# Gate and up of 17 of 22 feed-forward blocks in seven half-size products; the inner rows in four parts

## The chip, the cores and the metric

The kernel runs on one core of one Trainium2 chip. The metric is the device time of one launch in microseconds. A core has five engines that run side by side and meet through semaphores: TensorE (PE, matrix products; the loading of its weights is shown apart as PEld), VectorE (DVE), ScalarE (ACT), GpSimd (POOL) and SyncE (SP), which here issues nearly all transfers. Each takes its instructions in program order. TensorE writes its products into PSUM; Vector and Scalar read them there.

## The reference, cut to what matters

A decoder trunk of two layers, one with a convolution and one with attention, is run for 512 new prompt tokens and 8 x 8 sample tokens, 576 columns in all. Each layer ends in a gated feed-forward part, which is all that the change touches:

```python
def swiglu(x, g, w_gate_up, w_down):
    gu = rms_norm(x, g) @ w_gate_up
    return (jax.nn.silu(gu[..., :D_FF]) * gu[..., D_FF:]) @ w_down
```

The model width is 1024 (8 k-tiles of 128) and D_FF is 2816, 22 blocks of 128 inner rows. All data is float32. The prompt and the sample tokens go through the same weights.

## The kernel before, in words

Activations lie transposed: features on the 128 partitions, the N = 576 tokens in the free dimension, taken in two halves of HN = 288. TensorE multiplies in a faster reduced format, so each factor is split into a high part and the rest (`split`, L270: ScalarE copies x into hi, Vector subtracts to get lo), and each k-tile of a product is three matmuls, hi x hi, hi x lo, lo x hi (`mm3`, L227 to L230).

Weights come as a stream in the order of use (`specs`, L104). `w_load` (L110) starts a transfer into one of two raw buffers. `w_split` (L130) takes the oldest raw block and queues its splitting into whi and wlo, two buffers of each; `w_work` (L157) issues queued pieces to ScalarE (L140) and Vector (L141). `w_next` (L161) hands out the oldest split block, starts a load, puts out up to two background cache copies of 1 MB on SP (`bg_copy`, L180, on average 1.5 a call) and splits the next block. The order of the work on each engine is the order in which the program writes it: the kernel asks for a manual schedule and no planner moves anything.

`ffn` (L772) runs once per layer. In each of two halves, eleven blocks are multiplied: a gate product and an up product (`proj`, L274) of 8 k-tiles x 2 token halves x 3 matmuls = 48 matmuls each. The input uh/ul is x times its norm weight; the factor by token, `rs`, is known only after the first block, so every block's result is multiplied by it as it leaves PSUM:

```python
nc.vector.tensor_mul(halves(t), pg, halves(rs))      # L795
nc.scalar.activation(s, t, AF.Silu)                  # L797
nc.vector.tensor_mul(halves(t2), pu, halves(rs))     # L799
nc.vector.tensor_mul(t2, t2, s)                      # L800
split(hh[:, f], hl[:, f], t2)                        # hi on ScalarE, lo on Vector
```

Then the half's eight down products (11 k-tiles, 66 matmuls each) are added into the residual xT (L810). In the last half `after` prepares the next stage column tile by column tile: `x_fill` in layer 0, the transposed output `y_rows` in layer 1. PSUM is used as four tiles of two banks.

Of the kernel before, what the change touches and what calls it, by code (L numbers as in the profile page):

```python
# [34 lines left out]
KT = 8  # L35
# [4 lines left out]
N = S + NS  # L40
# [4 lines left out]
GH = 3072  # L45
DFF = 2816
FT = DFF // 128
TAPS = 31
EPS = 1e-6
SC = HD ** -0.5  # L50
# [40 lines left out]
def trunk(ctx: ExitStack, tc: tile.TileContext, I, O, dbg=None):  # L91
# [12 lines left out]
    def spec(ap, shape, scale=None):  # L104
        specs.append((ap, shape, scale))

    wstate = {"raw": [], "ready": [], "n": 0, "rate": 1.5, "lo": nc.vector, "cut": 4}
    BUFR, BUFH = 2, 2

    def w_load():  # L110
        if not specs:
            return
        ap, shape, scale = specs.pop(0)
        raw = wpool.tile([128, WSLOT], F32, tag="wraw", name="wraw", bufs=BUFR)
        n = int(np.prod(shape))
        v = raw[:, :n]
        if len(shape) == 2:
            v = v.rearrange("p (a b) -> p a b", a=shape[0])
        else:
            v = v.rearrange("p (a b c) -> p a b c", a=shape[0], b=shape[1])  # L120
        if len(shape) == 2:
            nc.sync.dma_start(v, ap)
        else:
            for j in range(shape[1]):
                nc.sync.dma_start(v[:, :, j], ap[j])
        wstate["raw"].append((raw, n, shape, scale))

    parts = []

    def w_split(cut=None):  # L130
# [5 lines left out]
        hi = wpool.tile([128, WSLOT], F32R, tag="whi", name="whi", bufs=BUFH)  # L136
        lo = wpool.tile([128, WSLOT], F32R, tag="wlo", name="wlo", bufs=BUFH)

        def plain(c):
            nc.scalar.activation(hi[:, c], raw[:, c], AF.Copy)  # L140
            wstate["lo"].tensor_sub(lo[:, c], raw[:, c], hi[:, c].bitcast(F32))  # L141

        def scaled(k, m):
            c = slice(k * m, (k + 1) * m)
            nc.scalar.activation(hi[:, c], raw[:, c], AF.Copy, scale=scale[:, k:k + 1])
            nc.vector.scalar_tensor_tensor(lo[:, c], raw[:, c], scale[:, k:k + 1],
                                           hi[:, c].bitcast(F32), op0=ALU.mult, op1=ALU.subtract)
# [12 lines left out]

    def w_next(lazy=False):  # L161
        w_work()
        while not wstate["ready"]:
            if not wstate["raw"]:
                w_load()
            w_split()
            w_work()
        r = wstate["ready"].pop(0)
        if not lazy:
            w_load()  # L170
        bg_copy()
        w_split()
        if not lazy:
            w_work()
        return r
# [11 lines left out]
    def col_blocks(w, k0, nk, c0, nc_):  # L187
        return w[k0 * 128:(k0 + nk) * 128, c0:c0 + nc_].rearrange("(k p) n -> p k n", p=128)
# [6 lines left out]

    def ffn_specs(l):
        wg, wd = I["w_gate_up"][l], I["w_down"][l]
        for hf in range(2):
            for f in range(hf * 11, hf * 11 + 11):
                spec([col_blocks(wg, 0, KT, f * 128, 128), col_blocks(wg, 0, KT, DFF + f * 128, 128)], (KT, 2, 128))  # L200
            for m in range(KT):
                spec(col_blocks(wd, hf * 11, 11, m * 128, 128), (11, 128))

    ffn_specs(0)

# [26 lines left out]
    def halves(ap):  # L232
        return ap.rearrange("p (h n) -> p h n", h=2)
# [36 lines left out]
    def split(hi, lo, x):  # L270
        nc.scalar.activation(hi, x, AF.Copy)  # L271
        nc.vector.tensor_sub(lo, x, hi.bitcast(F32))
# [499 lines left out]
    def ffn(l, u, before_last, after, late=0):  # L772
        with ExitStack() as cx:
            big = cx.enter_context(tc.tile_pool(name=f"f_big{l}", bufs=1))
            wk = cx.enter_context(tc.tile_pool(name=f"f_wk{l}", bufs=2))
            ps = cx.enter_context(tc.tile_pool(name=f"f_ps{l}", bufs=4, space=PSUM, reuse_waits="tile"))
            rs = big.tile([128, N], F32, name="rs")
            hh = big.tile([128, 11, N], F32R, name="hh")
            hl = big.tile([128, 11, N], F32R, name="hl")
            ks = [(k, k) for k in range(KT)]  # L780
            for hf in range(2):
                for f in range(11):
                    wh, wl = w_next()
                    if hf == 0 and f == 0:

                        pg, pu = (x[:, :, :HN] for x in pair(ps, [wh[:, :, i] for i in range(2)],
                                                             [wl[:, :, i] for i in range(2)], u.uh, u.ul))
                    else:
                        pg = proj(ps, wh, wl, u.uh, u.ul, ks, lambda w, k: w[:, k, 0])
                        pu = proj(ps, wh, wl, u.uh, u.ul, ks, lambda w, k: w[:, k, 1])  # L790
                    if hf == 0 and f == 0:
                        rstd_bc(ps, wk, u.acc, rs)
                        nc.scalar.activation(u.acc[:, 0:1], u.acc[:, 0:1], AF.Silu)
                    t = wk.tile([128, N], F32, name="gt")
                    nc.vector.tensor_mul(halves(t), pg, halves(rs))  # L795
                    s = wk.tile([128, N], F32, name="sg")
                    nc.scalar.activation(s, t, AF.Silu)  # L797
                    t2 = wk.tile([128, N], F32, name="gt2")
                    nc.vector.tensor_mul(halves(t2), pu, halves(rs))  # L799
                    nc.vector.tensor_mul(t2, t2, s)  # L800
                    split(hh[:, f], hl[:, f], t2)
                if hf:
                    u.close()
                    before_last()
                for m in range(KT):
                    wh, wl = w_next()
                    pt = proj(ps, wh, wl, hh, hl, [(k, k) for k in range(11)], lambda w, k: w[:, k])
                    if hf and late and m:
                        after(ps, wk, m - 1)
                    nc.vector.tensor_add(halves(xT[:, m]), halves(xT[:, m]), pt)  # L810
                    if hf and not late:
                        after(ps, wk, m)
                if hf and late:
                    after(ps, wk, KT - 1)


# [779 lines left out]
```

## Time and profile before

| | |
|---|---|
| median of 3 runs | 2066.39 us (2065.44 to 2069.13) |
| the profiled execution: its own time | 2061.0 us |
| its span, first to last instruction | 2059.1 us |
| mean granted TensorE clock | 0.98 |
| matmuls | 17109 |
| gate and up matmuls behind each layer's first block | 4032 (3 x 1344) |
| down matmuls | 2112 (3 x 704) |

The profile's first part gives each engine's busy time, share of the span and count. A group row gives line, engine, operation, output and inputs, shape and count, then the total busy time in us and the mean of one in ns, then the idle time before it and what ended it. A timeline row begins with its start in us from the start of the span and its length in us; matmuls overlap, so their length is not their pitch. A row of stretches gives, for each engine, the busy time and the number of instructions, then the clock, the DMA share and GB/s.

### The profile page before, as it was taken

Reading aid. Unit: us, or ns where it says so; the run is one execution under the profiler, and the core shown is the slowest. Engines: PE = TensorE matmul, PEld = TensorE weight load, DVE = VectorE, ACT = ScalarE, POOL = GpSimd, SP = SyncE. Lnnn points to the kernel's source line nnn. Section 1 sums busy time; section 2 is a strip of 40 time slices with the busy share of each in tenths; the row PEclk is TensorE's granted clock in tenths of the full one; section 3 lists DMA queues with packets and bytes.
Section 4 is the critical chain, followed back from the end, with each engine's and each line's share of the span. In section 5 each row is a group of like instructions: output and inputs, shape, how many; then the busy total and the mean of one; then the engine's idle time right before and its main releaser. Section 6 shows DMA issues by size and latency. Waiting matters only on the chain.

```text
span 2059.1 us, 40751 instructions
## 1 busy us (share of the span) xinstructions
PE 1950.8 (95%) x17109; PEld 1801.3 (87%) x17109; DVE 1013.1 (49%) x1922; ACT 810.7 (39%) x1836; POOL 159.9 (8%) x292
## 2 busy tenths in 40 slices
PE   6989799999999999999999999988897999999999
PEld 6767499999999999998888888866566999999998
DVE  5776665432444486564455356325454454324432
ACT  6554633221222343444344344266564332112221
POOL 1000000000000033130122032000112000000000
PEclk9999899999999999999999999989898999999999
DMA  7430196568655856759778887699979555643222
GB/s 211 144 143 22 34 322 224 197 213 292 204 197 189 290 165 198 212 171 259 209 212 230 246 230 211 205 227 220 205 160 249 202 203 197 217 117 82 76 71 75
DMA packets 368873, 387.81 MB, mean 188 GB/s; under 512 B 17983, under 2 KB 357975, under 8 KB 367010
## 3 DMA queue, kind: packets, MB, share of 16 engines
q1 hardware_dynamic: 368130, 384.06, 62.4%
q8 instruction: 135, 2.21, 0.5%
q0 software_dynamic: 560, 1.14, 0.2%
q14 instruction: 48, 0.39, 0.1%
HBM read 348.07 MB, written 146.86 MB: 240 GB/s over the span
## 4 chain that ended last, share of the span: by engine, by line
PE 84%; DMA 6%; ACT 5%; DVE 3%; SPq 1%; issue 1%; another core or an unknown queue 0%; ACTq 0%; DVEq 0%
PE pmm L230 13%; PE pmm L229 13%; PE pmm L228 13%; PE pj L228 7%; PE pj L229 7%; PE pj L230 7%; PE pj L1191 3%; PE tp L964 3%; PE acc L558 3%; PE pmp L229 2%; PE pmp L230 2%; PE pmp L228 2%; DMA nat<-scr 2%; PE pv L1062 2%; PE tp L989 2%; DMA vv<-in_cache_kv_w_dram 1%
## 5 line engine op out<-in xcount | busy, mean ns | idle before, releaser
L230 PE MATMUL pmm<-uh,wlo 128*128 128x288 f32 x1344 | 396.2, 295 | 0.0
L228 PE MATMUL pmm<-uh,whi 128*128 128x288 f32 x1344 | 395.9, 295 | 0.0
L229 PE MATMUL pmm<-ul,whi 128*128 128x288 f32 x1344 | 395.7, 294 | 0.0
L228 PE MATMUL pj<-whi,xh 128*128 128x256 f32 x1152 | 332.0, 288 | 0.9 <-DVE xT L810 0.9
L229 PE MATMUL pj<-wlo,xh 128*128 128x256 f32 x1152 | 322.3, 280 | 0.0
L230 PE MATMUL pj<-whi,xl 128*128 128x256 f32 x1152 | 322.1, 280 | 0.0
L228 PEld LDWEIGHTS pmm<-uh,whi 128*128 128x128 f32 x1344 | 252.1, 188 | 0.1
L229 PEld LDWEIGHTS pmm<-ul,whi 128*128 128x128 f32 x1344 | 252.1, 188 | 0.1
L230 PEld LDWEIGHTS pmm<-uh,wlo 128*128 128x128 f32 x1344 | 252.1, 188 | 0.0
L228 PEld LDWEIGHTS pj<-whi,xh 128*128 128x128 f32 x1152 | 217.2, 189 | 10.3 <-issue 9.5
L140 ACT ACTIVATE whi<-wraw 128x1024 fp32r<-128x1024 f32 (+3 forms) x206 | 169.2, 872 | 123.0 <-PE pmm L229 100.6
L229 PEld LDWEIGHTS pj<-wlo,xh 128*128 128x128 f32 x1152 | 217.2, 189 | 0.0
L230 PEld LDWEIGHTS pj<-whi,xl 128*128 128x128 f32 x1152 | 216.7, 188 | 0.0
L141 DVE TENSOR_TENSOR wlo<-wraw,whi 128x1024 fp32r<-128x1024 f32 (+3 forms) x206 | 197.7, 1003 | 23.3 <-ACT whi L140 23.0
L228 PE MATMUL pmm<-hh,whi 128*128 128x288 f32 x704 | 207.6, 295 | 0.0
L230 PE MATMUL pmm<-hh,wlo 128*128 128x288 f32 x704 | 207.5, 295 | 0.0
L229 PE MATMUL pmm<-hl,whi 128*128 128x288 f32 x704 | 207.2, 294 | 0.0
L799 DVE TENSOR_TENSOR gt<-pmm,rs 128x576 f32<-128x576 f32 x42 | 31.8, 757 | 224.6 <-PE pmm L230 224.6
L271 ACT ACTIVATE hh<-gt 128x576 fp32r<-128x576 f32 x44 | 30.2, 686 | 263.3 <-DVE gt L800 263.3
L229 PEld LDWEIGHTS pmm<-hl,whi 128*128 128x128 f32 x704 | 132.1, 188 | 0.0
L228 PEld LDWEIGHTS pmm<-hh,whi 128*128 128x128 f32 x704 | 132.1, 188 | 0.0
L230 PEld LDWEIGHTS pmm<-hh,wlo 128*128 128x128 f32 x704 | 132.0, 188 | 0.0
(295 smaller groups left out, 3518.3 us busy)
## 6 DMA issues: line engine op xcount, KB each, us to landing
out_dram<-in_cache_kv_w_dram SPq DMA_DIRECT2D x64, 1016.0 KB
wraw<-in_w_gate_up_dram SPq DMA_DIRECT2D x88, 512.0 KB
out_dram<-in_cache_kv_w_dram SPq DMA_DIRECT2D x32, 1008.0 KB
wraw<-in_w_kv_dram SPq DMA_DIRECT2D x24, 1024.0 KB
wraw<-in_w_down_dram SPq DMA_DIRECT2D x32, 704.0 KB
kk<-in_cache_kv_w_dram SPq DMA_DIRECT2D x40, 512.0 KB
vv<-in_cache_kv_w_dram SPq DMA_DIRECT2D x40, 512.0 KB
scr<-r SPq DMA_DIRECT2D x36, 512.0 KB
```

The lines of the kernel that those rows point to most:

```text
L140: nc.scalar.activation(hi[:, c], raw[:, c], AF.Copy)
L141: wstate["lo"].tensor_sub(lo[:, c], raw[:, c], hi[:, c].bitcast(F32))
L228: nc.tensor.matmul(out, wh, xh, start=start, stop=False)
L229: nc.tensor.matmul(out, wh, xl, start=False, stop=False)
L230: nc.tensor.matmul(out, wl, xh, start=False, stop=stop)
L271: nc.scalar.activation(hi, x, AF.Copy)
L558: nc.tensor.matmul(acc[r][32 * (j - m):32 * (j - m) + 32], DG[c][g, j], exf[c][g, j:S + j], start=m == 0, stop=j + 4 >= TAPS)
L799: nc.vector.tensor_mul(halves(t2), pu, halves(rs))
L964: nc.tensor.transpose(pt[:, j * 128:(j + 1) * 128], Z["k", n][:, j, i * 128:(i + 1) * 128], ident)
L989: nc.tensor.matmul(pt[32 * bi:32 * bi + 32, a:a + n], q[:, x, i, b], kn[:, x, i, T * b:T * b + T] if k is None else k[:, i, bi], start=i = ...
L1062: nc.tensor.matmul(pvt[r], ph[:n, ti, r], v[:n, bi], start=ti == 0, stop=ti == 9)
L1191: nc.tensor.matmul(pt[:, :CW], xs[:, k], x[:, k], start=k == 0 and x is wh, stop=k == KT - 1 and x is wl)
```

## The change

The weight matrix of a block is seen as 2 x 2: gate and up by k-tiles 0 to 3 and 4 to 7; the input as 2 x 2: k-tiles 0 to 3 and 4 to 7 by token halves h0 and h1. The four results (gate and up, h0 and h1) are formed from seven products of half size, 12 matmuls each, in place of eight. Four sums of weight blocks and four sums of input blocks go into them. Partial results are shared by leaving them in a PSUM bank, copying the bank to SBUF with ScalarE (p1, p5, u2, u3) and adding the next product into the same bank.

The 22 blocks of a layer become quarters of 5, 6, 6 and 5, each followed by its own part of the down products, and so hh and hl hold six blocks in place of eleven. The first quarter runs as before (`plain`); beside its blocks 1 to 4 the input sums th/tl are made. The sums mix token halves, so the input has to carry `rs` beforehand: beside the first quarter's down products `rescale` rewrites uh and ul. The other 17 blocks run as `seven`. A weight block then splits into seven pieces of 512 columns, four in one pair of buffers and three (`w_tail`) in the next, so one block takes both pairs. Down weights come as nf k-tiles by 256 columns, two output tiles a load. The lo parts of hh are kept pending in `pend` and issued by `flush`.

```diff
+QUARTERS = [(0, 5), (5, 6), (11, 6), (17, 5)]
...
+    def w_tail():
+
+        if wstate["tail"] is not None:
+            w_work()
+            raw, sw, e = wstate["tail"]
+            wstate["tail"] = None
+            hi, lo = w_slot()
+            split(hi[:, :1024], lo[:, :1024], sw[:, 1024:])
+            split(hi[:, 1024:1536], lo[:, 1024:1536], raw[:, 1536:])
+            e += [hi, lo]
...
+        if scale == "seven":
+
+            r = [raw[:, i * 512:(i + 1) * 512] for i in range(4)]
+            sw = wstate["sums"]()
+            t = [sw[:, i * 512:(i + 1) * 512] for i in range(4)]
+            add, sub = nc.vector.tensor_add, nc.vector.tensor_sub
+            parts.extend([partial(add, t[0], r[2], r[3]), partial(sub, t[1], t[0], r[0]), partial(sub, t[2], r[0], r[2]),
+                          partial(sub, t[3], r[1], t[1]),
+                          partial(split, hi[:, :1024], lo[:, :1024], raw[:, :1024]),
+                          partial(split, hi[:, 1024:], lo[:, 1024:], sw[:, :1024])])
+            e = [hi, lo]
+            wstate["tail"] = (raw, sw, e)
+            wstate["ready"].append(e)
+            return
...
+    def w_take():
+
+        w_work()
+        r = wstate["ready"].pop(0)
+        w_load()
+        bg_copy()
+        return r
...
+        for f0, nf in QUARTERS:
+            for f in range(f0, f0 + nf):
+                spec([col_blocks(wg, 0, KT, f * 128, 128), col_blocks(wg, 0, KT, DFF + f * 128, 128)], (2, KT, 128),
+                     "seven" if f0 else None)
+            for m in range(0, KT, 2):
+                spec(col_blocks(wd, f0, nf, m * 128, 256), (nf, 256))
...
+            def input_sums(j):
+                za = wk.tile([128, N], F32, tag="sg", name="za")
+                zb = wk.tile([128, N], F32, tag="gt2", name="zb")
+                normed(za, j, slice(0, N))
+                normed(zb, j + 4, slice(0, N))
+                t = sums_tile()[:, :4 * HN].rearrange("p (a b) -> p a b", a=4)
+                nc.vector.tensor_sub(t[:, 0], za[:, h1], za[:, h0])
+                nc.vector.tensor_sub(t[:, 1], zb[:, h1], t[:, 0])
+                nc.vector.tensor_sub(t[:, 2], zb[:, h1], za[:, h1])
+                nc.vector.tensor_sub(t[:, 3], zb[:, h0], t[:, 1])
+                nc.scalar.activation(th[:, :, j], t, AF.Copy)
+                pend.append(lambda: nc.vector.tensor_sub(tl[:, :, j], t, th[:, :, j].bitcast(F32)))
+
+            def rescale(ks):
+
+                for k in ks:
+                    c = h0 if k < 4 else slice(0, N)
+                    z = wk.tile([128, N], F32, tag="sg", name="zs")
+                    normed(z[:, c], k, c)
+                    nc.scalar.activation(u.uh[:, k, c], z[:, c], AF.Copy)
+                    flush()
+                    pend.append(lambda k=k, c=c, z=z: nc.vector.tensor_sub(u.ul[:, k, c], z[:, c],
+                                                                           u.uh[:, k, c].bitcast(F32)))
+                flush()
...
+            def seven(i):
+
+                wxh, wxl, wyh, wyl = w_take()
...
+                direct(a, wxh, wxl, 0, 0, h0, True, False)
+                nc.scalar.activation(sn["p1"], a, AF.Copy)
+                direct(b, wxh, wxl, 1, 4, h0, True, True)
+                nc.vector.tensor_add(s[:, h0], sn["p1"], b)
+                nc.scalar.activation(s[:, h0], s[:, h0], AF.Silu)
+                summed(c, wxh, wxl, 2, 0, True, False)
+                nc.scalar.activation(sn["p5"], c, AF.Copy)
+                summed(a, wxh, wxl, 3, 1, False, False)
+                nc.scalar.activation(sn["u2"], a, AF.Copy)
+                w_split()
+                w_work(4 if wstate["tail"] is not None else 0)
+                flush()
+                w_work(1)
+                summed(a, wyh, wyl, 0, 2, False, False)
+                nc.scalar.activation(sn["u3"], a, AF.Copy)
+                nc.vector.tensor_add(t2[:, h1], sn["u3"], sn["p5"])
+                w_work()
+                direct(c, wyh, wyl, 1, 4, h1, False, True)
+                nc.vector.tensor_add(s[:, h1], sn["u2"], c)
+                nc.scalar.activation(s[:, h1], s[:, h1], AF.Silu)
+                summed(a, wyh, wyl, 2, 3, False, True)
+                nc.vector.tensor_mul(t2[:, h1], t2[:, h1], s[:, h1])
+                nc.vector.tensor_mul(t2[:, h0], s[:, h0], a)
+                w_tail()
+                nc.scalar.activation(hh[:, i], t2, AF.Copy)
+                pend.append(lambda: nc.vector.tensor_sub(hl[:, i], t2, hh[:, i].bitcast(F32)))
...
+                if last:
+                    flush()
+                    tpool.__exit__(None, None, None)
                     u.close()
                     before_last()
-                for m in range(KT):
+                for m0 in range(0, KT, 2):
                     wh, wl = w_next()
...
+                    flush()
+                    if not q:
+
+                        rescale([[0, 1], [2, 3, 4], [5, 6, 7], []][m0 // 2])
+                    for m in (m0, m0 + 1):
+                        pt = proj(ps, wh, wl, hh, hl, [(k, k) for k in range(nf)],
+                                  lambda w, k: w[:, k, 128 * (m - m0):128 * (m - m0) + 128])
...
+                        nc.vector.tensor_add(halves(xT[:, m]), halves(xT[:, m]), pt)
...
+                    w_tail()
```

`direct` multiplies the input itself and `summed` the input sums; both issue 12 matmuls, four k-tiles of three.

More of the change, by code (lines that the diff above doesn't have):

```diff
@@ L105, in spec @@
         specs.append((ap, shape, scale))
-    wstate = {"raw": [], "ready": [], "n": 0, "rate": 1.5, "lo": nc.vector, "cut": 4}
+    wstate = {"raw": [], "ready": [], "n": 0, "rate": 1.5, "lo": nc.vector, "cut": 4, "tail": None}
     BUFR, BUFH = 2, 2
@@ L123, in w_load, with w_slot @@
         else:
-            for j in range(shape[1]):
-                nc.sync.dma_start(v[:, :, j], ap[j])
+            for j, a in enumerate(ap):
+                nc.sync.dma_start(v[:, j] if shape[0] == 2 else v[:, :, j], a)
         wstate["raw"].append((raw, n, shape, scale))
     parts = []
+    def w_slot():
+        return [wpool.tile([128, WSLOT], F32R, tag=t, name=t, bufs=BUFH) for t in ("whi", "wlo")]
+    def w_tail():
[7 more added lines that the diff above has]
+            e += [hi, lo]
     def w_split(cut=None):
@@ L135, in w_split @@
         raw, n, shape, scale = wstate["raw"].pop(0)
-        hi = wpool.tile([128, WSLOT], F32R, tag="whi", name="whi", bufs=BUFH)
-        lo = wpool.tile([128, WSLOT], F32R, tag="wlo", name="wlo", bufs=BUFH)
+        hi, lo = w_slot()
+        if scale == "seven":
[11 more added lines that the diff above has]
+            return
         def plain(c):
@@ L197, in ffn_specs @@
         wg, wd = I["w_gate_up"][l], I["w_down"][l]
-        for hf in range(2):
-            for f in range(hf * 11, hf * 11 + 11):
-                spec([col_blocks(wg, 0, KT, f * 128, 128), col_blocks(wg, 0, KT, DFF + f * 128, 128)], (KT, 2, 128))
-            for m in range(KT):
-                spec(col_blocks(wd, hf * 11, 11, m * 128, 128), (11, 128))
+        for f0, nf in QUARTERS:
[4 more added lines that the diff above has]
+                spec(col_blocks(wd, f0, nf, m * 128, 256), (nf, 256))
     ffn_specs(0)
@@ L776, in ffn @@
             ps = cx.enter_context(tc.tile_pool(name=f"f_ps{l}", bufs=4, space=PSUM, reuse_waits="tile"))
+            tpool = tc.tile_pool(name=f"f_t{l}", bufs=1, side="right", reuse_waits="tile")
+            tp = tpool.__enter__()
             rs = big.tile([128, N], F32, name="rs")
-            hh = big.tile([128, 11, N], F32R, name="hh")
-            hl = big.tile([128, 11, N], F32R, name="hl")
+            hh = big.tile([128, 6, N], F32R, name="hh")
+            hl = big.tile([128, 6, N], F32R, name="hl")
@@ L780, in ffn @@
+            th = tp.tile([128, 4, 4, HN], F32R, name="th")
+            tl = tp.tile([128, 4, 4, HN], F32R, name="tl")
             ks = [(k, k) for k in range(KT)]
[L781 to L787, printed above, removed]
-                    else:
[L789 to L802, printed above, removed]
@@ new lines, in ffn, with flush, sums_tile, normed @@
+            h0, h1 = slice(0, HN), slice(HN, N)
+            pend = []
+            def flush():
+                while pend:
+                    pend.pop(0)()
+            def sums_tile():
+                return big.tile([128, 2048], F32, tag="sw", name="sw")
+            wstate["sums"] = sums_tile
+            def normed(z, k, c):
+                nc.vector.scalar_tensor_tensor(z, xT[:, k, c], u.g[:, k:k + 1], rs[:, c], op0=ALU.mult, op1=ALU.mult)
+            def input_sums(j):
[10 more added lines that the diff above has]
+                pend.append(lambda: nc.vector.tensor_sub(tl[:, :, j], t, th[:, :, j].bitcast(F32)))
@@ new lines, in plain @@
+            def plain(f):
+                wh, wl = w_next()
+                flush()
+                if f == 0:
+                    pg, pu = (x[:, :, :HN] for x in pair(ps, [wh[:, i] for i in range(2)], [wl[:, i] for i in range(2)],
+                                                         u.uh, u.ul))
+                    rstd_bc(ps, big, u.acc, rs)
+                    nc.scalar.activation(u.acc[:, 0:1], u.acc[:, 0:1], AF.Silu)
+                else:
+                    pg = proj(ps, wh, wl, u.uh, u.ul, ks, lambda w, k: w[:, 0, k])
+                    pu = proj(ps, wh, wl, u.uh, u.ul, ks, lambda w, k: w[:, 1, k])
+                s = wk.tile([128, N], F32, name="sg")
+                nc.vector.tensor_mul(halves(s), pg, halves(rs))
+                nc.scalar.activation(s, s, AF.Silu)
+                t2 = wk.tile([128, N], F32, name="gt2")
+                nc.vector.tensor_mul(halves(t2), pu, halves(rs))
+                nc.vector.tensor_mul(t2, t2, s)
+                split(hh[:, f], hl[:, f], t2)
+                if f:
+                    input_sums(f - 1)
@@ new lines, in seven, with product, direct, summed @@
+            def seven(i):
+                wxh, wxl, wyh, wyl = w_take()
+                pa = ps.tile([128, 2, 512], F32, tag="mm", name="pwa")
+                pc = ps.tile([128, 2, 512], F32, tag="mm", name="pwc")
+                a, b, c = pa[:, 0, :HN], pa[:, 1, :HN], pc[:, 0, :HN]
+                sn = {x: big.tile([128, HN], F32, tag=x, name=x) for x in ("p1", "p5", "u2", "u3")}
+                s = wk.tile([128, N], F32, name="sg")
+                t2 = wk.tile([128, N], F32, name="gt2")
+                def product(out, wh, wl, blk, xh, xl, start, stop):
+                    for j in range(4):
+                        w = slice(blk * 512 + j * 128, blk * 512 + j * 128 + 128)
+                        for n, (x, y) in enumerate(((wh, xh), (wh, xl), (wl, xh))):
+                            nc.tensor.matmul(out, x[:, w], y(j), start=start and j + n == 0, stop=j == 3 and n == 2,
+                                             skip_group_check=True)
+                def direct(out, wh, wl, blk, o, h, start, stop):
+                    product(out, wh, wl, blk, lambda j: u.uh[:, o + j, h], lambda j: u.ul[:, o + j, h], start, stop)
+                def summed(out, wh, wl, blk, n, start, stop):
+                    product(out, wh, wl, blk, lambda j: th[:, n, j], lambda j: tl[:, n, j], start, stop)
+                direct(a, wxh, wxl, 0, 0, h0, True, False)
[24 more added lines that the diff above has]
+                pend.append(lambda: nc.vector.tensor_sub(hl[:, i], t2, hh[:, i].bitcast(F32)))
@@ L803, in ffn @@
+            for q, (f0, nf) in enumerate(QUARTERS):
+                last = q == len(QUARTERS) - 1
+                for i in range(nf):
+                    if q:
+                        seven(i)
+                    else:
+                        plain(i)
+                if last:
+                    flush()
+                    tpool.__exit__(None, None, None)
                     u.close()
                     before_last()
-                for m in range(KT):
+                for m0 in range(0, KT, 2):
@@ L806, in ffn @@
                     wh, wl = w_next()
[L807 to L813, printed above, removed]
+                    flush()
+                    if not q:
+                        rescale([[0, 1], [2, 3, 4], [5, 6, 7], []][m0 // 2])
@@ new lines, in ffn @@
+                    for m in (m0, m0 + 1):
+                        pt = proj(ps, wh, wl, hh, hl, [(k, k) for k in range(nf)],
+                                  lambda w, k: w[:, k, 128 * (m - m0):128 * (m - m0) + 128])
+                        if last and late and m:
+                            after(ps, wk, m - 1)
+                        nc.vector.tensor_add(halves(xT[:, m]), halves(xT[:, m]), pt)
+                        if last and not late:
+                            after(ps, wk, m)
@@ L814, in ffn @@
+                    w_tail()
+                if last and late:
                     after(ps, wk, KT - 1)
```

## The prediction, made before the changed kernel ran

> **What bounds the kernel now.** I read the engine totals and the chain of waits first, then each feed-forward stretch by itself, since only those change.
>
> ```profile
> PE 1950.8 (95%) x17109; PEld 1801.3 (87%) x17109; DVE 1013.1 (49%) x1922; ACT 810.7 (39%) x1836; POOL 159.9 (8%) x292
> ...
> PE 84%; DMA 6%; ACT 5%; DVE 3%; SPq 1%; issue 1%; another core or an unknown queue 0%; ACTq 0%; DVEq 0%
> ```
>
> TensorE carries 84% of the chain. Next the stretches: gate and up of layer 0's first eleven blocks (306.60 on), its down products (433.90 on), and the end of layer 0 (643.00 on). Columns: busy us of PE, weight loads, DVE, ACT, POOL with counts, then clock, DMA share, GB/s.
>
> ```profile
> 306.60:433.90 127.30, 127.30 (x962) 127.25 (x961) 56.60 (x65) 38.28 (x47) 0.00 (x0) 1.00 0.63 217
> 433.90:505.00 71.10, 71.10 (x539) 71.10 (x539) 22.12 (x27) 13.92 (x19) 0.00 (x0) 1.00 0.75 256
> 643.00:717.00 74.00, 73.06 (x555) 72.86 (x554) 34.10 (x57) 25.16 (x48) 0.00 (x0) 1.00 0.76 263
> ```
>
> TensorE never idles there at clock 1.00; DVE is 44% busy (56.60 of 127.30), DMA has room. So a matmul removed here is time removed, and any bubble put into TensorE is time added. The first row holds ten blocks of 96 matmuls: 127.30 / 960 = 0.1326 us each, the pitch.
>
> **What is removed.** Each of 17 blocks per layer goes from 96 to 84 matmuls (seven products of 4 k-tiles x 3). 2 x 17 x 12 = 408 matmuls x 0.1326 = **54.1 us**. The down products keep 22 x 8 x 2 x 3 matmuls a layer. The mean durations of 294 ns in the page overlap and aren't the price.
>
> The Trainium skill ("TensorE: Matmul & The Clock Gate", "Back-to-back issue gap") gives N/2.4 + 2.5 ns, 122.5 ns for 288 columns; by it the saving would be 50.0 us. The row's 132.6 ns decides; this trace doesn't agree with the page's figure.
>
> **What is added inside a block.** Product 4 adds into bank `a`, ScalarE copies it (u2), and product 5 adds into the same bank at once: TensorE must wait for that copy. The other copies (p1, p5, u3) have one or two whole products (12 x 0.1326 = 1.59 us each) before their bank is written again. One wait of this kind, a 288-column PSUM copy that TensorE waits for, is in the trace:
>
> ```profile
> L600 ACT ACTIVATE pil<-inp x2: 383/385/387, 122.2 to 122.5; 128x288 f32<-128x288 f32 x2
> ...
> 122.24 0.68 ACT L600 ACTIVATE pil<-inp 128x288 f32<-128x288 f32 x2
> 122.67 0.61 PE L228 MATMUL inp<-uh,whi 128*128 128x288 f32 x1 [3.38 <-ACT pil L600]
> 123.08 0.44 PE L229 MATMUL inp<-ul,whi 128*128 128x288 f32 x1
> 123.32 0.44 PE L230 MATMUL inp<-uh,wlo 128*128 128x288 f32 x1
> ...
> 126.42 0.30 PE L228 MATMUL inp<-uh,whi 128*128 128x288 f32 x1
> 126.55 0.29 PE L229 MATMUL inp<-ul,whi 128*128 128x288 f32 x1
> ```
>
> The first copy ends at 122.24 + 0.385, the matmul starts 0.05 later. Its 0.61 against 0.44 afterwards says that its own weights still loaded, some 0.17. And the reader's side, at the end of layer 0's eleventh block:
>
> ```profile
> 433.87 0.29 PE L230 MATMUL pmm<-uh,wlo 128*128 128x288 f32 x1
> 434.00 0.29 PE L228 MATMUL pmm<-hh,whi 128*128 128x288 f32 x1
> ...
> 434.20 0.76 DVE L799 TENSOR_TENSOR gt<-pmm,rs 128x576 f32<-128x576 f32 x1 [5.60 <-PE pmm L230]
> 435.06 0.76 DVE L800 TENSOR_TENSOR gt<-gt,sg 128x576 f32<-128x576 f32 x1
> 435.86 0.69 ACT L271 ACTIVATE hh<-gt 128x576 fp32r<-128x576 f32 x1 [6.48 <-DVE gt L800]
> 436.58 0.76 DVE L272 TENSOR_TENSOR hl<-gt,hh 128x576 fp32r<-128x576 f32 x1 [0.76 <-ACT hh L271]
> 437.26 0.89 DVE L141 TENSOR_TENSOR wlo<-wraw,whi 128x704 fp32r<-128x704 f32 x1
> ```
>
> A reader starts 0.33 after the last matmul's start. So from that start to the next matmul: 0.33 + 0.385 + 0.05 + 0.13 (weights, warm; an estimate under the cold 0.17) = 0.89, less the normal 0.13: **0.76 us a block, 34 x 0.76 = 25.8 us**. Bounds: 0.6 if the weights load ahead of the wait, 1.0 with a 0.49 us copy (the sigmoid below) and cold weights: 20 to 34 us. It can't be nothing: the next product writes the bank that is being read. Behind the waiting product stand products 5 to 7 and all later TensorE work; ScalarE's u3 and Vector's gate sum wait for them, with nothing else to do. A block is then 84 x 0.1326 + 0.76 = 11.90 us against 12.73.
>
> **Do Vector and Scalar keep up?** Rows for their new work (mean ns is the number before the second bar):
>
> ```profile
> L141 DVE TENSOR_TENSOR wlo<-wraw,whi 128x1024 fp32r<-128x1024 f32 x102 | 120.4, 1222 | 11.1 <-ACT whi L140 10.9
> L140 ACT ACTIVATE whi<-wraw 128x1024 fp32r<-128x1024 f32 x102 | 101.7, 1045 | 28.6 <-PE pmm L229 28.0 <-DMA wraw<-in_a_w_out_dram 0.6
> L141 DVE TENSOR_TENSOR wlo<-wraw,whi 128x704 fp32r<-128x704 f32 x64 | 54.1, 887 | 6.9 <-ACT whi L140 6.9
> L140 ACT ACTIVATE whi<-wraw 128x704 fp32r<-128x704 f32 x64 | 46.9, 781 | 87.4 <-PE pmm L229 72.6 <-issue 14.8
> L141 DVE TENSOR_TENSOR wlo<-wraw,whi 128x512 fp32r<-128x512 f32 x32 | 19.9, 684 | 2.4 <-ACT whi L140 2.4
> L140 ACT ACTIVATE whi<-wraw 128x512 fp32r<-128x512 f32 x32 | 17.4, 617 | 0.0
> L268 DVE SCALAR_TENSOR_TENSOR ul<-xT,cols,uh 128x576 fp32r<-128x576 f32 x16 | 13.1, 818 | 13.5 <-ACT uh L267 13.5
> L531 ACT ACTIVATE sg<-inp,cols 128x288 f32<-128x288 f32 x14 | 6.8, 487 | 2.8 <-PE inp L230 2.8
> L538 DVE SCALAR_TENSOR_TENSOR ext<-inp,cols,sg 128x288 f32<-128x288 f32 x7 | 3.6, 512 | 0.4 <-PE inp L230 0.3
> L810 DVE TENSOR_TENSOR xT<-xT,pmm 128x576 f32<-128x576 f32 x32 | 24.1, 754 | 173.5 <-PE pmm L230 173.5
> L146 DVE SCALAR_TENSOR_TENSOR wlo<-wraw,cols,whi 128x256 fp32r<-128x256 f32 x288 | 121.6, 480 | 16.1 <-ACT whi L145 16.1
> ...
> 324.45 2.36 DVE L141 TENSOR_TENSOR wlo<-wraw,whi 128x1024 fp32r<-128x1024 f32 x2 [0.19 <-ACT whi L140]
> ```
>
> Sizes between rows are read off the line through 512 and 1024 columns, 1.05 ns a column on Vector and 0.84 on Scalar: 288 columns 0.45, 640 0.82, 768 0.95, 1152 1.36 on Vector; 768 0.84 and 1152 1.15 on Scalar.
>
> Vector, per block of seven: four weight sums of 512 (0.69), lo parts of 1024 three times (1.22) and 512 once, five operations of 288 (0.45 to 0.51), hl 0.76: 2.75 + 4.35 + 2.4 + 0.76 = 10.3 us of 11.90, 86%. Scalar: 3 x 1.045 + 0.62 + 4 x 0.385 + 2 x 0.45 + 0.69 = 6.9 us. Walking the in-order queues: the block's last multiply waits for product 7, then the last lo parts end 3.3 us into the next block, its four sums 6.5, the first lo after hi (which stands behind u2) 9.2, the second 11.5, before the block ends. u2 stands behind p1, the first silu and p5 on ScalarE; that silu waits for a Vector addition behind those lo parts. It could start 1.9 us later before u2 were late, so nothing on the path.
>
> In the five ordinary blocks the new input sums (2 x 0.82 + 4 x 0.45, then 1.15 on ScalarE and 1.36 on Vector) make the circle sums, split, multiply, hl about 12.7 us, as long as TensorE's block: no cost taken, up to 1 us late at the last. The rescaling of uh and ul, 8 x 1.0 to 1.6 us, lies beside the first quarter's down products (4 x 60 x 0.1326 = 31.8 us); Vector is full there but by my walk each weight is ready 0.6 to 3 us before its use. The 32 additions into xT a layer in place of 16 (0.75 each) lie beside down products of 4 us and more; four PSUM tiles give each two more products' time.
>
> **Boundaries.** Down products now begin on hh after 5 or 6 k-tiles, not 11. Before, hl stands complete at 437.34 (436.58 + 0.76), 3.34 after 434.00, and k-tile 10 needs it at 31 x 0.1326 = 4.1: hidden. Now:
> - After the ordinary quarter: k-tile 4 needs hl at 13 x 0.1326 = 1.72; same chain 3.34 + 0.05 + 0.11: **1.8 us**, twice: 3.6.
> - After quarters 2 and 3: the last hl is kept pending, and the next weight's two lo parts of 768 (0.95 each, waiting for hi behind hh) are issued ahead of it on Vector. After the last product: multiply to 0.66, hh to 1.39, hi to 2.23, lo to 4.18, hl to 4.94; k-tile 5 needs it at 16 x 0.1326 = 2.12. With restart **3.0 us**, four times: 12.0. If that order didn't hold, 0.2; if the weight or its buffer comes late, 4 or more.
> - Before the last down products the pending hl is flushed first: 2.36 against 1.72: 0.64, twice: 1.3.
> - Layer 0's last two tiles: Vector's work for them and the next stage's weight split ahead of it (8 x 0.48 = 3.8 us) barely fit their 60 x 0.1326 = 7.95 us: 1.0 taken, 0 to 3.
>
> **DMA.** Loads keep their number and bytes a layer (44 of half a block, 16 of down weights, now 5 or 6 k-tiles by 256 columns in place of 11 by 128). A block moves the same bytes in 11.90 instead of 12.73 us: 217 GB/s becomes 232, share 0.63 to 0.67. A load is issued about 12 us before its first reader. SP's copies are unchanged in number. I cost it at nothing; without that cover each late weight would hold Scalar, Vector and then TensorE.
>
> **Sum:** -54.1 + 25.8 + 3.6 + 12.0 + 1.3 + 1.0 = **-10.4 us**. The profiled execution took 2061.0 us (span 2059.1, 1.9 around it): 2050.6 for it. The runs' median is 2066.4, 5.4 above that execution; the same change on the median is **2056.0**.
>
> **Rivals.**
> - *Cheap bubbles.* The restart waits for no weights (0.6) and hl isn't late (0.2 instead of 3.0): -54.1 + 20.4 + 3.6 + 0.8 + 1.3 + 1.0 = -27: 2039. For it: weight loads overlap matmuls all through the trace. Against: the order of the code.
> - *A wash.* The bubble is 1.0 us and boundaries a little dearer: -54.1 + 34 + 18 = -2: 2064.
> - *Vector becomes the bound.* Place: the in-order circle sums, lo, addition, silu, multiply, lo, some 10.7 us with its handoffs. If it takes 20% longer (12.9 us), the first silu and then u2 slide with it and every block costs 12.9 - 11.9 = 1.0 us more: 34 us, 2090. It decides from a block time of 12.2 us, where 34 x (12.73 - 12.2) only pays for the 18 us of boundaries. Against: no row of before shows Vector over half busy in these stretches, and like operations back to back overlap by about 0.08 us (two lo's of 1024 take 2.36, not 2.44). For: the gap 434.96 to 435.06 shows dependent operations 0.1 apart.
> - *The clock falls.* After the idle 3.38 us above, matmuls came 0.24 apart for 3.5 us: some 15 x 0.11 = 1.6 us lost. If every u2 bubble did this: 34 x 1.6 = 54 us, 2110. Against: the idle there was four times as long as a bubble.
>
> The Trainium skill ("TensorE: Matmul & The Clock Gate", "A second HAM failure mode: psum-queue depth-cycling") says that micro-idles between matmul groups can make the clock oscillate, which is this last rival; here the three stretches hold clock 1.00 but have no such idles.
>
> **How the numbers follow.** Forecast 45%, cheap bubbles 17%, wash 17%, Vector 18%, clock 3%. About 0.2% (4 us) can be told from no change. Of the forecast's 45, 3 fall within that and 42 are faster; cheap bubbles are all faster; of the wash 4 are faster, 11 the same, 2 slower; of Vector's 18, 3 are the same and 15 slower. Faster 42 + 17 + 4 = 0.63, same 3 + 11 + 3 = 0.17, slower 2 + 15 + 3 = 0.20. The forecast's own range is 2045 to 2066; the range 2036 to 2082 takes in the bubble's and boundaries' bounds and half of Vector's case.
>
> **What would show it.** Blocks of 84 matmuls about 11.9 us apart; one wait per block, 34 in all, of TensorE on the 128x288 copy into u2, 0.7 to 0.8 us each; four waits of about 3 us on hl at the first down product of quarters 2 and 3 in each layer; Vector 80 to 90% busy in those stretches, never the releaser at a block's first product; clock 1.00. I am wrong if blocks take over 12.2 us, if TensorE waits for whi or wlo inside quarters, or if the hl waits are missing.

## The result and the profile after

| | before | after |
|---|---|---|
| median of the runs side by side, 4 each | 2067.57 us (2065.44 to 2069.13) | 2102.98 us (2096.78 to 2105.19) |
| span of the profiled execution | 2059.1 us | 2102.6 us |
| mean granted clock | 0.980 | 0.979 |
| matmuls | 17109 | 16701 |

The changed kernel is slower: the ratio after to before is 1.0167, with a 95% interval of 1.0141 to 1.0193. The forecast was 2056.0 us, with a range from 2036 to 2082. So the prediction was wrong, and on the wrong side.

The 408 matmuls are gone and yet the time grew. To see where, I cut both executions at marks that both have: the matmuls `pst` stand just ahead of each layer's feed-forward part, and the matmuls `tp<-ones,xacc` just behind the first one. These are rows of one tile each (shortest, median and longest duration in ns, then the start in us of the first and of the last). The kernel before:

```profile
L253 PE MATMUL pst<-acc,ones x8: 403/405/406, 305.8 to 1642.0; 128*128 128x288 f32 x8
L861 PE MATMUL tp<-ones,xacc x10: 164/250/250, 717.7 to 718.6; 128*128 128x1 f32 x8, 128*64 128x1 f32 x2
```

The changed kernel:

```profile
L290 PE MATMUL pst<-acc,ones x8: 403/405/406, 311.1 to 1665.6; 128*128 128x288 f32 x8
L1010 PE MATMUL tp<-ones,xacc x10: 166/250/250, 742.7 to 743.7; 128*128 128x1 f32 x8, 128*64 128x1 f32 x2
```

| stretch | before | after | difference |
|---|---|---|---|
| ahead of layer 0's feed-forward part (unchanged work) | 305.8 | 311.1 | +5.3 |
| layer 0's feed-forward part | 411.9 | 431.6 | +19.7 |
| between the two (unchanged work) | 924.3 | 922.9 | -1.4 |
| layer 1's feed-forward part, to the end | 417.1 | 437.0 | +19.9 |

The loss lies in the two changed parts, 39.6 us of the 43.5 between the spans. The first part of the page (busy time of each engine) and the chain of waits show its kind:

```profile
PE 1923.2 (91%) x16701; PEld 1753.2 (83%) x16701; DVE 1225.6 (58%) x2314; ACT 935.9 (45%) x2098; POOL 162.0 (8%) x292
...
PE 74%; ACT 11%; DVE 7%; DMA 5%; issue 2%; SPq 1%; another core or an unknown queue 0%; ACTq 0%; DVEq 0%
```

TensorE is busy for 27.6 us less (1950.8 to 1923.2), but its share of the chain of waits went from 84% to 74%, and ScalarE's from 5% to 11%. The list of TensorE's waits names what it stands for (the line that waits, the line that lets it go; total us, times, longest):

```profile
PE pwa L899 <- ACT p L909: 34.0, 34, 1.1
PE pwa L899 <- ACT u L916: 19.0, 34, 0.8
PE pmm L266 <- DVE hl L933: 11.1, 6, 2.6
...
PE pj L265 <- DVE xT L958: 1.9, 1, 1.9
PE pmm L265 <- ACT hh L308: 1.7, 2, 0.9
...
PE pmm L266 <- DVE hl L309: 0.8, 2, 0.4
```

The second row is the u2 bubble that was forecast, 34 times. The first row, the largest, was forecast at nothing: TensorE waits in every block for p1, the first copy. One block in the timeline of TensorE (start, length, then in brackets the idle time ahead):

```profile
410.66 0.29 PE L899 MATMUL pwa<-uh,wlo 128*128 128x288 f32 x1
412.06 0.40 PE L899 MATMUL pwa<-uh,whi 128*128 128x288 f32 x1 [1.11 <-ACT p L909]
412.29 0.29 PE L899 MATMUL pwa<-ul,whi 128*128 128x288 f32 x1
...
417.65 0.40 PE L899 MATMUL pwa<-th,whi 128*128 128x288 f32 x1 [0.56 <-ACT u L916]
```

And ScalarE at the same place:

```profile
411.04 0.67 ACT L932 ACTIVATE hh<-gt 128x576 fp32r<-128x576 f32 x1
411.61 0.39 ACT L909 ACTIVATE p<-pwa 128x288 f32<-128x288 f32 x1
```

Product 1 puts its last matmul out at 410.66. Product 2, which writes the other bank `b`, starts at 412.06, right behind the end of the copy of bank `a` (411.61 + 0.39 = 412.00). The copy itself is late because it stands in ScalarE's queue behind hh of the block before. The idle times understate the cost: start to start there are 1.40 us in place of 0.13, and the first matmul behind the gap takes 0.23 to the next, 0.10 more than the pitch. So a wait costs its idle time and 0.26 more, here 1.37 us.

Not all of this comes from the wait as such. In the first block of each quarter no hh stands ahead of the copy, and there the wait is shorter, six times in the kernel:

```profile
398.77 0.40 PE L899 MATMUL pwa<-uh,whi 128*128 128x288 f32 x1 [0.50 <-ACT p L909]
```

With the 0.26 that is 0.76 us, the price that the prediction gave to a copy in TensorE's way. The other 28 blocks pay 0.61 more, because the copy is late.

The block period follows from the start of the same Vector row in blocks four apart:

```profile
414.01 0.45 DVE L911 TENSOR_TENSOR sg<-p,pwa 128x288 f32<-128x288 f32 x1 [1.53 <-PE pwa L899]
...
467.41 0.45 DVE L911 TENSOR_TENSOR sg<-p,pwa 128x288 f32<-128x288 f32 x1 [1.53 <-PE pwa L899]
```

(467.41 - 414.01) / 4 = 13.35 us a block, against 96 x 0.1326 = 12.73 before and 11.90 forecast. It is above the 12.2 us that the prediction gave as the point of being wrong.

### The profile page after: what moved, and what is told of

Read it like the earlier page. It is cut to its first block, busy times and chain, and to the rows that moved or that the text cites. A ratio compares the mean times of both kernels' runs of the same rounds, so it can differ in the third digit from the quotient of the medians.

```text
span 2102.6 us, 40703 instructions
## 1 busy us (share of the span) xinstructions
PE 1923.2 (91%) x16701; PEld 1753.2 (83%) x16701; DVE 1225.6 (58%) x2314; ACT 935.9 (45%) x2098; POOL 162.0 (8%) x292
## 4 chain that ended last, share of the span: by engine, by line
PE 74%; ACT 11%; DVE 7%; DMA 5%; issue 2%; SPq 1%; another core or an unknown queue 0%; ACTq 0%; DVEq 0%
PE pwa L899 9%; PE pj L265 7%; PE pj L266 6%; PE pj L267 6%; PE pmm L266 6%; PE pmm L267 6%; PE pmm L265 6%; ACT whi L308 3%; PE pj L1340 3%; PE tp L1113 3%; PE pwc L899 3%; PE acc L595 3%; PE pmp L266 2%; PE pmp L267 2%; PE pmp L265 2%
## 5 line engine op out<-in xcount | busy, mean ns | idle before, releaser
L265 PEld LDWEIGHTS pj<-whi,xh 128*128 128x128 f32 x1152 | 217.1, 188 | 11.2 <-issue 10.4
L266 PE MATMUL pmm<-hl,whi 128*128 128x288 f32 x704 | 210.3, 299 | 11.9 <-DVE hl L933 11.1
L169 DVE TENSOR_TENSOR wlo<-wraw,whi 128x512 fp32r<-128x512 f32 (+4 forms) x138 | 118.0, 895 | 54.7 <-ACT whi L168 54.3
L899 PE MATMUL pwa<-th,whi 128*128 128x288 f32 x408 | 123.9, 304 | 19.0 <-ACT u L916 19.0
L168 ACT ACTIVATE whi<-wraw 128x512 fp32r<-128x512 f32 (+4 forms) x138 | 101.9, 786 | 81.8 <-PE pmm L266 74.3
L174 DVE SCALAR_TENSOR_TENSOR wlo<-wraw,cols,whi 128x256 fp32r<-128x256 f32 x288 | 121.6, 483 | 16.1 <-ACT whi L173 16.1
L173 ACT ACTIVATE whi<-wraw,cols 128x256 fp32r<-128x256 f32 x288 | 123.7, 498 | 0.0
L899 PE MATMUL pwa<-tl,whi 128*128 128x288 f32 x408 | 120.4, 295 | 0.0
L899 PE MATMUL pwa<-th,wlo 128*128 128x288 f32 x408 | 120.2, 295 | 0.0
L958 DVE TENSOR_TENSOR xT<-xT,pmm 128x576 f32<-128x576 f32 x64 | 47.6, 751 | 121.6 <-PE pmm L267 121.5
L899 PE MATMUL pwa<-uh,whi 128*128 128x288 f32 x272 | 83.6, 307 | 34.0 <-ACT p L909 34.0
L1113 PE MATMUL tp<-ident,kk 128*128 128x128 f32 x576 | 90.9, 285 | 15.2 <-ACT kt L1122 6.5
```

The source lines that it names most:

```text
L265: nc.tensor.matmul(out, wh, xh, start=start, stop=False)
L266: nc.tensor.matmul(out, wh, xl, start=False, stop=False)
L899: nc.tensor.matmul(out, x[:, w], y(j), start=start and j + n == 0, stop=j == 3 and n == 2, skip_group_check=True)
L1113: nc.tensor.transpose(pt[:, j * 128:(j + 1) * 128], Z["k", n][:, j, i * 128:(i + 1) * 128], ident)
```

## The experiments

The banks in question: `pa` is one PSUM tile of two banks; `a` is its first bank, `b` its second; `c` is the first bank of another tile, `pc`. Three explanations of the wait for p1 stood against each other. *By tile*: the wait that the program sets covers the whole PSUM tile, so that a product into `b` waits for a reader of `a`, though the banks differ. *By the copy*: TensorE can't write PSUM while ScalarE copies the bank that it has just left, whatever tile the next product writes. *By Vector*: Vector with its extra work sets the block period, and the waits of TensorE only show it.

**Bank b in a tile of its own.**

```diff
-                a, b, c = pa[:, 0, :HN], pa[:, 1, :HN], pc[:, 0, :HN]
+                pb = ps.tile([128, 2, 512], F32, tag="mm", name="pwb")
+                a, b, c = pa[:, 0, :HN], pb[:, 0, :HN], pc[:, 0, :HN]
```

> The changed kernel with one edit: the second product's bank b lies in a PSUM tile of its own instead of the second half of a's tile. Theory 1 (the wait covers the whole PSUM tile: product 2 waits for ScalarE's copy of bank a only because b is in the same tile): the 34 waits on p1 go (34.0 us of idle time and about 0.26 us of restart each, 43 us), those on u2 stay at 0.56 us; blocks of seven 13.3 us apart become 11.9 to 12.0; 2103 becomes 2060, about the time of the kernel before. Theory 2 (TensorE can't go on to any bank while ScalarE copies the bank it has just left): the 34 waits stay, 2103. Theory 3 (Vector is the limit once that wait is gone): waits on p1 go, but blocks settle above 12.4 us and TensorE waits on u2 longer than 0.56 us: 2075 to 2090.

Measured: 2061.3 us (2060.27 to 2064.93), 0.997 of the kernel before (0.9957 to 0.9983). The span is 2059.2 us. TensorE's waits in layer 0 (300 to 735 us), and Vector's row four blocks apart:

```profile
PE pwa L900 <- ACT u L917: 9.6, 17, 0.8
PE pmm L266 <- DVE hl L934: 5.6, 3, 2.6
```

```profile
410.42 0.46 DVE L912 TENSOR_TENSOR sg<-p,pwb 128x288 f32<-128x288 f32 x1 [0.16 <-PE pwb L900]
...
458.33 0.45 DVE L912 TENSOR_TENSOR sg<-p,pwb 128x288 f32<-128x288 f32 x1 [0.16 <-PE pwb L900]
```

The wait for p1 is gone, and a block takes 47.91 / 4 = 11.98 us: 1.37 less, just the cost read above. The copy itself is still there and just as late. The timeline of both engines shows it beside product 2:

```profile
409.36 0.29 PE L900 MATMUL pwb<-uh,whi 128*128 128x288 f32 x1
409.39 0.39 ACT L910 ACTIVATE p<-pwa 128x288 f32<-128x288 f32 x1
409.49 0.29 PE L900 MATMUL pwb<-ul,whi 128*128 128x288 f32 x1
409.62 0.29 PE L900 MATMUL pwb<-uh,wlo 128*128 128x288 f32 x1
```

While ScalarE reads `a`, the matmuls into `pwb` come every 0.13 us as ever. So the explanation by the copy falls. Vector has the same work as in the changed kernel, and the period fell all the same, so Vector wasn't what held it at 13.35. The wait is one that the program sets: in the changed kernel as built, the first matmul of product 2 waits for a semaphore of ScalarE, and in this one it does not.

**The order of two products turned round as well.** The bubble for u2 comes from product 5 adding into the bank that u2 copies right behind product 4. With product 4 ahead of product 3 (into `c`), each copy has a whole product to be made in.

```diff
+                summed(a, wxh, wxl, 3, 1, False, False)
+                nc.scalar.activation(sn["u2"], a, AF.Copy)
                 summed(c, wxh, wxl, 2, 0, True, False)
                 nc.scalar.activation(sn["p5"], c, AF.Copy)
-                summed(a, wxh, wxl, 3, 1, False, False)
-                nc.scalar.activation(sn["u2"], a, AF.Copy)
```

> As e1_b_own_tile, and products 3 and 4 change places, so that the third product into bank a no longer follows the second at once: the copy u2 has a whole product (1.59 us) of cover. Theory 1: the waits on u2 go too (19.0 us idle and 34 x 0.26 of restart, 28 us): 2032, blocks 11.1 to 11.2 us apart. Theory 2: the copies still hold up whatever comes next: no gain over e1_b_own_tile. Theory 3 (Vector, 10.3 us of work a block, becomes the bound): blocks at 11.6 to 12 us, TensorE waits for whi or wlo or a late silu, 2045 to 2060.

Measured, both edits together: 2035.69 us (2032.54 to 2041.49), 0.9849 of the kernel before (0.9826 to 0.9871). Vector's row four blocks apart, and a stretch of blocks (us, then busy us and count for PE, weight loads, DVE, ACT, POOL, then clock, DMA share, GB/s):

```profile
406.98 0.45 DVE L912 TENSOR_TENSOR sg<-p,pwb 128x288 f32<-128x288 f32 x1 [0.16 <-PE pwb L900]
...
451.62 0.46 DVE L912 TENSOR_TENSOR sg<-p,pwb 128x288 f32<-128x288 f32 x1 [0.16 <-PE pwb L900]
```

```profile
412.00:460.00 48.00, 48.00 (x363) 48.00 (x362) 37.96 (x58) 26.53 (x47) 0.00 (x0) 1.00 0.61 214
```

44.64 / 4 = 11.16 us: 0.82 less again, and as good as 84 x 0.1326 = 11.14. TensorE has no gap left in these blocks, Vector is 79% busy (37.96 of 48.00), and it lets TensorE wait nowhere. This also measures two terms alone: u2 costs 11.98 - 11.16 = 0.82 us a block, and the twelve matmuls spared are worth 12.73 - 11.16 = 1.57.

**The pending lo parts ahead of the next weight.** What remains is the wait of 2.6 us for hl at the first down products of quarters 2 and 3. The weight's two lo parts stand ahead of hl on Vector, and this edit puts hl first.

```diff
                 for m0 in range(0, KT, 2):
+                    if q:
+                        flush()
                     wh, wl = w_next()
```

> As e2_b_own_tile_order, and from the second quarter on the pending lo part of hh is issued ahead of the next down weight's split instead of behind it. Theory of the prediction (the last hl stands behind two lo parts of the weight in Vector's queue): four waits of 2.6 us become 0.4 to 0.6, 9 to 10 us less than e2_b_own_tile_order: 2022. Rival (TensorE is then held by the weight that comes later instead): no gain over e2_b_own_tile_order.

Measured, all three edits: 2026.5 us (2018.93 to 2030.24), 0.9792 of the kernel before (0.9766 to 0.9818). It is faster than both kernels. The first place and the waits in layer 0:

```profile
464.54 0.76 DVE L934 TENSOR_TENSOR hl<-gt,hh 128x576 fp32r<-128x576 f32 x1 [0.75 <-ACT hh L933]
465.27 1.83 DVE L169 TENSOR_TENSOR wlo<-wraw,whi 128x768 fp32r<-128x768 f32 x2
```

```profile
PE pj L265 <- DVE xT L961: 1.9, 1, 1.9
...
PE pmm L266 <- DVE hl L934: 0.3, 1, 0.3
```

hl now runs ahead of the two lo parts on Vector, and of the three waits for it in layer 0, 5.6 us in all, one of 0.3 is left, the one before the last down products. The two feed-forward parts take 391.3 and 393.8 us, against 411.9 and 417.1 before. From the second experiment to this one they shrank by 6.5 and 7.9 us, 14.4 in all, in the profiled executions. At each of the four places the step from one matmul to the next went from 2.89 or 2.90 us to 0.42, which makes 4 x 2.47 = 9.9. The rest is the clock, told of in the last section: four falls of 1.5 us went with the waits, and one came elsewhere. The medians differ by 9.2.

**Bank b beside c.** The explanation by tile asks more: moved to the second bank of `pc`, product 2 should be free of p1, and product 3, which writes `c`, should wait for Vector's reading of `b`.

```diff
-                a, b, c = pa[:, 0, :HN], pa[:, 1, :HN], pc[:, 0, :HN]
+                a, b, c = pa[:, 0, :HN], pc[:, 1, :HN], pc[:, 0, :HN]
```

> The changed kernel with bank b in the second half of c's tile instead of a's. Theory 1 (the wait covers the tile): no wait on p1 any more; instead product 3, which writes c, waits for Vector's addition that reads b, some 0.33 + 0.45 us after product 2, idle 0.6 us or more a block, up to 2 us where Vector is late. Theory 2: waits on p1 as before, and none of product 3 on Vector.

Measured, in a single run: 2100.68 us, span 2098.6. TensorE's largest wait in layer 0, and Vector's row four blocks apart:

```profile
PE pwc L899 <- DVE sg L911: 10.5, 17, 0.6
```

```profile
413.08 0.46 DVE L911 TENSOR_TENSOR sg<-p,pwc 128x288 f32<-128x288 f32 x1 [0.16 <-PE pwc L899]
...
464.50 0.45 DVE L911 TENSOR_TENSOR sg<-p,pwc 128x288 f32<-128x288 f32 x1 [0.16 <-PE pwc L899]
```

The wait moved to the product whose tile now holds `b`, with another engine as the reader, 17 times in 17 blocks. A block takes 51.42 / 4 = 12.85 us, so this wait costs 12.85 - 11.98 = 0.87. Summed over the kernel, the 42.8 us that p1 costs (34.0 us of idle time and 34 x 0.26) become 21.0 + 34 x 0.26 = 29.8, 13.0 less. The feed-forward parts took 428.0 and 429.0 us, 3.6 and 8.0 less than in the changed kernel, 11.6 together. Beside the waits the clock fell once more than in the changed kernel (two more in layer 0, one fewer in layer 1; last section), and 13.0 - 1.5 = 11.5. The single time shows only 2.3 us less, because the unchanged work between the two parts took 7 us more than in the changed kernel. I have no cause for that.

**The order alone.** With `b` back beside `a`, turning the order round should take away the wait for u2 and bring one for Vector's reading of `b`, in front of product 4. This product goes on adding into `a` and opens no new sum; if only the opening of a sum made TensorE wait for the other bank, it would run on.

```diff
+                summed(a, wxh, wxl, 3, 1, False, False)
+                nc.scalar.activation(sn["u2"], a, AF.Copy)
                 summed(c, wxh, wxl, 2, 0, True, False)
                 nc.scalar.activation(sn["p5"], c, AF.Copy)
-                summed(a, wxh, wxl, 3, 1, False, False)
-                nc.scalar.activation(sn["u2"], a, AF.Copy)
```

> The changed kernel with only products 3 and 4 exchanged; b stays in a's tile. Product 4, which now follows product 2 at once, adds into a and so doesn't open a new group. Theory 1 (the wait covers the tile, whatever the product): the wait on p1 stays (1.37 us a block), the one on u2 goes (0.82), and a new one comes: product 4 waits for Vector's addition that reads b (0.87 us a block by the run with b beside c): blocks about 13.4 us apart, no gain, 2100 to 2105. Rival (only a product that opens a new group waits for the tile's readers): no wait of product 4 on Vector, blocks 12.5 us, 2075.

Measured, in a single run: 2109.17 us, beside 2068.63 for the kernel before; span 2107.1. The two largest waits in layer 0 and one block of TensorE's timeline:

```profile
PE pwa L899 <- ACT p L909: 17.2, 17, 1.4
PE pwa L899 <- DVE sg L911: 10.5, 17, 0.6
```

```profile
409.49 0.40 PE L899 MATMUL pwa<-uh,whi 128*128 128x288 f32 x1 [1.11 <-ACT p L909]
...
411.96 0.40 PE L899 MATMUL pwa<-th,whi 128*128 128x288 f32 x1 [0.62 <-DVE sg L911]
```

Product 4 waits 0.62 us for Vector, though it opens no sum. The wait goes by the tile, whatever the product does with it. (Each of these tiles is one pair of neighbouring banks, so no run here tells the tile from the pair.) The order that gains 0.82 us a block when `b` has its own tile gains nothing without it: a block takes 13.41 us against 13.35, by the same Vector row. The two feed-forward parts took 2.3 us more than in the changed kernel; the rest of the longer time lies in unchanged work.

## Why the prediction was wrong

**The step that failed** is in the part on what is added inside a block: "The other copies (p1, p5, u3) have one or two whole products (12 x 0.1326 = 1.59 us each) before their bank is written again." The sentence is right about banks, and the wait goes by tiles. Product 2 writes the same tile right behind product 1, so p1 has no product at all to hide behind. The price of 0 was in truth 34.0 us of idle time and 34 x 0.26 for the restarts, 42.8 us. Of this 34 x 0.76 = 25.8 is a second copy in TensorE's way, as dear as u2 was forecast, and some 28 x 0.61 = 17 comes from hh ahead of the copy on ScalarE, an order that the prediction's walk of ScalarE's queue did not name. The code quoted beside the prediction showed `a` and `b` in one tile; I never asked by what unit the program sets its waits. The bounds and the range had no room for it, since the rivals priced u2, the boundaries, Vector and the clock, and none a second copy in the path.

The Trainium skill ("PSUM — Partial Sum Buffer", "Summary: rules for kernel authors") says that PSUM may be read while a matmul runs if the two touch different banks. The first experiment agrees, with matmuls 0.13 us apart beside the 0.39 us copy of the other bank; the changed kernel kept to that rule and paid 0.76 to 1.37 us a block all the same.

The other steps, one by one:

| step | forecast | measured |
|---|---|---|
| 408 matmuls | -54.1 | -53.4 (34 x 1.57) |
| u2 | +25.8 (20 to 34) | +27.8 (19.0 + 34 x 0.26) |
| p1 | 0 | +42.8 |
| after ordinary quarter | +3.6 | +3.5 (1.7 + 0.8 + 4 x 0.26) |
| after quarters 2 and 3, and before the last down products | +13.3 | +12.7 (11.1 + 6 x 0.26) |
| layer 0's end | +1.0 | +1.0 (a wait of 1.9, before 0.9) |
| the clock | 0 | +4.6 (three falls, last section) |
| sum | -10.4 | +39.0 |

The two parts measure +39.6 between the marks, so hardly anything is left unexplained there. Without the row p1 the sum is -3.8. The first experiment, which has no such wait, agrees: its two parts took 411.7 and 415.5 us, 1.8 less than before, and its clock fell once more than the changed kernel's, so that -3.8 + 1.5 = -2.3 is to be compared. Its median is 6.3 us below the kernel before (2061.3 against 2067.6). The forecast of -10.4 was thus too good even for a kernel without this wait, by some 4 us in the medians.

The 122.5 ns beside which the prediction set its pitch are, in the section of the Trainium skill that it cites, the gap of a matmul taken by itself. The row of 132.6 ns is a stream with a weight load to every matmul, so the two do not contradict each other.

**The boundaries** came as walked through. The timeline of the changed kernel at the end of quarter 2:

```profile
476.82 0.69 ACT L932 ACTIVATE hh<-gt 128x576 fp32r<-128x576 f32 x1 [0.89 <-DVE gt L930]
477.41 1.56 ACT L168 ACTIVATE whi<-wraw 128x768 fp32r<-128x768 f32 x2
478.27 1.83 DVE L169 TENSOR_TENSOR wlo<-wraw,whi 128x768 fp32r<-128x768 f32 x2 [1.49 <-ACT whi L168]
480.02 0.75 DVE L933 TENSOR_TENSOR hl<-gt,hh 128x576 fp32r<-128x576 f32 x1
480.82 0.40 PE L266 MATMUL pmm<-hl,whi 128*128 128x288 f32 x1 [2.60 <-DVE hl L933]
```

hh, hi, both lo parts and only then hl: TensorE loses 2.60 + 0.26 = 2.86 us, where 3.0 was forecast. The third experiment takes the order away and the wait with it.

**Vector as the bound** (18%) fell: in the second experiment's blocks it is 79% busy and TensorE waits for nothing. Its work there is 0.79 x 11.16 = 8.8 us a block, where 10.3 were forecast. **The clock** (3%) did fall behind idle times, but not behind the bubbles of every block that this rival named, as the last section shows. **The transfers** cost nothing that can be seen; no weight is among the waits inside the blocks. The other two cases, cheap bubbles and a wash, were about sizes that are now measured, and neither had p1 in it.

What stays open: why unchanged stretches differ by 5 to 10 us between profiled executions (the part ahead of layer 0's feed-forward part took 305.8 us before and 311.1 after). The medians therefore carry the verdicts, and the waits and periods the causes.

## What to carry to other kernels

Before a copy out of PSUM is priced at nothing, ask which tile the next product writes, not which bank: give every bank that is read on its own a tile of its own. Then order the products so that a copy of a bank always has a whole product into another tile to hide behind; here the two edits together turned a loss of 1.7% into a gain of 1.5%. Where work waits in a list to be issued later, look at what is issued ahead of it on the same engine when the list is emptied.

## What the runs showed of the hardware

The clock fell after short idle times, at the same place in one kernel and not in another. These are four stretches of the changed kernel (columns as in the stretches above), each behind a wait of 2.60 us for hl at the first down products of a quarter, and one with the bubbles of p1 and u2:

```profile
480.80:486.00 5.20, 5.17 (x39) 5.18 (x40) 0.75 (x1) 0.00 (x0) 0.00 (x0) 1.00 0.94 341
601.30:606.50 5.20, 4.94 (x25) 4.94 (x26) 0.70 (x2) 0.00 (x0) 0.00 (x0) 0.67 0.86 311
1834.00:1839.00 5.00, 4.39 (x21) 4.39 (x22) 0.55 (x1) 0.00 (x0) 0.00 (x0) 0.66 0.51 156
1956.00:1961.00 5.00, 4.38 (x21) 4.38 (x22) 0.57 (x1) 0.00 (x0) 0.00 (x0) 0.66 0.50 157
...
412.00:460.00 48.00, 42.38 (x305) 40.76 (x306) 33.95 (x50) 21.68 (x40) 0.00 (x0) 1.00 0.62 213
```

In three of the four the granted clock is 0.66 or 0.67, in the first it is 1.00. TensorE's timeline at the second:

```profile
602.64 0.44 PE L267 MATMUL pmm<-hh,wlo 128*128 128x288 f32 x1
602.88 0.44 PE L265 MATMUL pmm<-hh,whi 128*128 128x288 f32 x1
...
605.76 0.39 PE L265 MATMUL pmm<-hh,whi 128*128 128x288 f32 x1
```

From 602.64 to 605.76, 3.1 us, matmuls come 0.24 us apart. From the first to the last matmul of such a quarter's down products 42.46 us pass with a fall (596.68 to 639.14) and 40.93 without (475.95 to 516.88), so a fall costs 1.5 us, and three cost the 4.6 of the table. The other kernels show the same after their waits of 2.60 us: the clock fell in 4 of 4 places in the second experiment, and in 3 of 4 in the first, the fourth and the fifth. That makes 16 of 20. The place spared is the first in the changed kernel and in the fifth experiment, the second in the first, and the third in the fourth. The third experiment took the idle time away there, and the falls with it: these stretches take 38.45 us, near 287 x 0.1326 = 38.06. Yet a fall came at the end of layer 0, behind the wait of 1.87 us:

```profile
697.37 0.36 PE L265 MATMUL pj<-whi,xh 128*128 128x256 f32 x1 [1.87 <-DVE xT L961]
...
698.73 0.41 PE L267 MATMUL pj<-whi,xl 128*128 128x256 f32 x1
698.94 0.41 PE L265 MATMUL pj<-whi,xh 128*128 128x256 f32 x1
```

There these matmuls, otherwise 0.12 apart, come every 0.21 us. With this wait of 1.86 or 1.87 us the clock fell in the first, the third and the fourth experiment, and not in the changed kernel, the second and the fifth: 3 of 6. So the account of the third experiment closes: 9.9 + 4 x 1.5 - 1.5 = 14.4.

The Trainium skill ("TensorE: Matmul & The Clock Gate", "The HAM clock gate") says that the clock drops after at least one idle window of about 3.4 us. Here it dropped after idle times of 2.60 and 1.87 us, in most cases or in half of them, so the trace doesn't agree with that figure as a lower limit. Nor does it with the rule weighed as a rival, that short idle times make the clock swing, at the lengths of the bubbles: with a gap of 1.11 and one of 0.56 us in every block, the last row of the stretches holds clock 1.00. What decides whether an idle time of 1.9 or 2.6 us counts was not settled.

A wait also costs more than its idle time in the profile: 0.26 us more for each, by p1 (1.37 against 1.11) and by u2 (0.82 against 0.56) alike.
